# Weight sums of the folded products made by accumulating DMAs in DRAM, with signs that need only additions

## The chip, the cores and the metric

The kernel runs on one core of a Trainium2 chip. The metric is the device time of one execution in microseconds (us). The kernel before takes 1085.0 us, the median of three runs (1084.67 to 1085.46). Profiles show one execution; its lines name TensorE as PE (its weight loads as PEld), VectorE as DVE, ScalarE as ACT, GpSimd as POOL and SyncE as SP, which issues nearly all DMAs.

## The reference

One layer of an encoder on 512 tokens with 1024 channels, all in float32. The part that the change concerns comes last:

```
mixed = (g_ssd * y_ssd + g_attn * y_attn) @ w_o          # (512, 1024) @ (1024, 1024)
x = x + rmsnorm(mixed, post_mix_norm)
h = rmsnorm(x, pre_mlp_norm)
f = square(relu(h @ w_mlp_in)) @ w_mlp_out               # (512, 1024) @ (1024, 4096), (512, 4096) @ (4096, 1024)
x = x + rmsnorm(f, post_mlp_norm)
```

Before it stand an input projection, a state-space scan over 8 groups of heads in both directions (`ssd`), an attention over a window of 128 tokens either way, gates, and the two output projections of these branches.

## The kernel before, in words

**Products.** Activations are kept transposed, channels on the 128 partitions and 512 tokens along the row. For accuracy each float32 operand is split into a high part in the matmul's reduced format and a low part (what is left), and every product is made of three matmuls: high by high, high by low, low by high (`mm3`, L404, `mm`, L398). ACT makes the high part of a weight by a cast, and POOL or DVE the low part by a subtraction (L473 and L477 for weights that are used as they are; L1571 and L1575 in `fold`).

**Quanta.** The work is a list of quanta, in order. An ordinary quantum is one block of 128 output channels: 8 blocks of the sum by 3 matmuls of 128x512, 24 matmuls. Each has its weight chunk of 512 KB, which SP loads (L453) into one of three raw buffers `wr`; the parts go into rings `wh` and `wl`, three deep (`SPL`). `prefetch` (L481) splits and loads ahead. Anything else is hung on a position in this list by `at(q, fn)` (L427): q is the index of a quantum, and a half means behind it. Tiles of 128x512 come from a common store of 67 slots (`Slots`).

**Order.** The program is first written down in this order. Then a planner (`Planner`, L77) simulates it with a duration for each instruction (`duration`, L205), a serial DMA queue (`plan`, L264) and the dependencies between tiles (`depend`, L156), and fixes the order of each engine's instructions (`chain`, L498). TensorE takes what is first in the list and ready; the others take what is due first. An instruction that was written down through `held_back` (L1341) may not start before the matmul ahead of it in the list has started. The semaphores make each engine wait, in its order, for what it really needs.

**Folded products.** The output projection w_o (`mix_quanta`, L1366) and each quarter of the down projection of the MLP (`down_quanta`, L1604; four parts of 1024 rows) are products of 2 x 2 blocks. They are made with seven block products instead of eight, by a scheme of Strassen and Winograd: sums S1 to S4 of activation blocks (`mix_second`, L1276; `combine`, L1457) meet sums T1 to T4 of weight blocks of 512x512, and three groups of products, X, Y and Z, are accumulated in PSUM and added up into the output (`done`). Before, the weight sums are T3 = B22 − B12, T2 = T3 + B11, T1 = B22 − T2, T4 = B21 − T2, written over the raw tiles where they can be:

```
sub(r("B12"), r("B22"), r("B12"))
add(r("B11"), r("B12"), r("B11"))
...
sub(raw[n, k], *((r("B22"), r("B11")) if n == "T1" else (r("B21"), r("B11"))))
```

DVE makes them, for tiles of 128 rows. For the down parts `fold` (L1522) does so when an operand is due (`operand`, L1539): it loads the four blocks B11, B12, B21, B22 of a part once, 16 tiles of 256 KB, keeps them in slots until their last use, and makes 16 adds or subtracts (L1536, L1537). For w_o `stage_wo` (L1347) does so beforehand, in four steps hung on the quanta of the scan branch's output projection (`ssd_out_quanta`): 16 loads, 16 adds or subtracts (L1358 to L1361) and 16 stores of the sums into DRAM tiles `wot`; `fold` then loads the seven operands of w_o one by one.

**Stages in time.** To about 618 us: input projection, attention and scan, with gates and the attention's output projection between them. To about 690 us: the scan's output projection. To 744 us: w_o. Then the residual, norms and transposes (`mix_done`, `flip_h2`), under which the MLP begins: `up_halves` makes the first three blocks of the up projection for one half of the tokens and then for the other. From about 765 us ordinary up quanta, from about 793 us up quanta and folded down quanta in turn. From 1037 us the last folded products alone, and from 1070 us the last vector work and the stores.

Of the kernel before, what the change touches and what calls it, by code (L numbers as in the profile page):

```python
# [37 lines left out]
FETCH, STAGE = 2, 1  # L38
# [38 lines left out]
class Planner:  # L77
# [78 lines left out]
    def depend(self):  # L156
        self.pre = [set() for _ in self.ins]
        live, users, ring, seen, first, base = {}, {}, {}, {}, {}, {}
        self.turn = [set() for _ in self.ins]
        for n, i in enumerate(self.ins):  # L160
            for write, aps in ((False, i.ins), (True, i.outs)):
                for ap in self.operands(aps):
# [15 lines left out]
                    key = (name, ap.offset, tuple(map(tuple, ap.ap)))  # L178
# [26 lines left out]
    def duration(self, n):  # L205
# [22 lines left out]
        if e == "POOL":  # L228
            if "pow" in str(getattr(i, "op", "")):
# [34 lines left out]
    def plan(self, wait=0.3):  # L264
# [12 lines left out]
        for _ in self.ins:  # L277
# [21 lines left out]
            if e == "SP":  # L299
# [39 lines left out]
class Trunk:  # L339
# [936 lines left out]
    def mix_second(self, k):  # L1276
# [5 lines left out]
        tt(s[:, hi], b[:, hi], a[:, hi], op=ALU.add)  # L1282
# [4 lines left out]
        tt(t[:, hi], b[:, lo], s[:, lo], op=ALU.subtract)  # L1287
# [59 lines left out]
    def stage_wo(self, k):  # L1347

        nc = self.nc
        b = {}  # L1350
        for i in range(2):
            for j in range(2):
                b[i, j] = self.slots.get("wd")
                r0 = (4 * i + k) * 128
                nc.sync.dma_start(b[i, j], self.d_w_o[0, r0:r0 + 128, j * 512:(j + 1) * 512])
        t2, t1 = self.slots.get("wd"), self.slots.get("wd")
        tt = nc.vector.tensor_tensor
        tt(b[0, 1], b[1, 1], b[0, 1], op=ALU.subtract)  # L1358
        tt(t2, b[0, 1], b[0, 0], op=ALU.add)
        tt(t1, b[1, 1], t2, op=ALU.subtract)  # L1360
        tt(b[1, 0], b[1, 0], t2, op=ALU.subtract)  # L1361
        for n, t in (("T1", t1), ("T2", t2), ("T3", b[0, 1]), ("T4", b[1, 0])):
            nc.sync.dma_start(self.wot[n][k * 128:(k + 1) * 128], t)
        self.slots.put(t1, t2, *b.values())

    def mix_quanta(self):  # L1366
# [9 lines left out]
        def done(t, j, ps, _):  # L1376
# [11 lines left out]
    def mix_done(self, t, h2):  # L1388
# [6 lines left out]
        for j in range(2):  # L1395
            nc.scalar.activation(junk, h2[j], AF.Square, accum_out=ssq[:, j:j + 1])
            nc.vector.tensor_tensor(h2[j], h2[j], self.g2[j], op=ALU.mult)
# [59 lines left out]
    def combine(self, part, k):  # L1457
# [16 lines left out]
        tt(s[:, hi], b[:, hi], a21, op=ALU.add)  # L1474
# [3 lines left out]
        tt(t[:, hi], b[:, lo], s[:, lo], op=ALU.subtract)  # L1478
# [43 lines left out]
    def fold(self, steps, src, ops, held, done, lo, tags, staged=None):  # L1522
# [5 lines left out]
        uses = {"B11": ["B11"], "T2": ["B22", "B12", "B11"], "T1": ["B22", "B11"], "T4": ["B21", "B11"], "T3": ["B12"],  # L1528
                "B22": ["B22"], "B21": ["B21"]}
        if staged:  # L1530
            uses = {n: [n] for n in uses}
        order = [s[1] for s, _ in steps]
        at = lambda x: [i for i, n in enumerate(order) if x in uses[n]]
        need = {n: [x for x in uses[n] if order[at(x)[0]] == n] for n in order}
        over = {n: tuple(x for x in uses[n] if order[at(x)[-1]] == n) for n in order}
        sub = lambda c, a, b: nc.vector.tensor_tensor(c, a, b, op=ALU.subtract)  # L1536
        add = lambda c, a, b: nc.vector.tensor_tensor(c, a, b, op=ALU.add)  # L1537

        def operand(n, k):  # L1539

            r = lambda x: raw[x, k]
            free = over[n]
            if staged:
                return r(n), free
            if n == "T2":
                sub(r("B12"), r("B22"), r("B12"))
                add(r("B11"), r("B12"), r("B11"))
            if n in ("T1", "T4"):
                raw[n, k] = get("wt")
                sub(raw[n, k], *((r("B22"), r("B11")) if n == "T1" else (r("B21"), r("B11"))))  # L1550
                free += n,
            return r({"T2": "B11", "T3": "B12"}.get(n, n)), free

        def chunk(n, c):
            ks = 2 * c, 2 * c + 1

            def loads():
                for x in need[n]:
                    for k in ks:
                        raw[x, k] = get("wd")  # L1560
                        nc.sync.dma_start(raw[x, k], staged[x][k * 128:(k + 1) * 128] if x[0] == "T" else
                                          src(int(x[1]) - 1, int(x[2]) - 1, k))

            def make(ring):
# [3 lines left out]
                for i, k in enumerate(ks):  # L1568
                    w, free = operand(n, k)
# [6 lines left out]
                    put(*[raw.pop((x, k)) for x in free])  # L1576
# [5 lines left out]
        def product(a, b, bank, after, last):  # L1582

            def run(parts):
# [3 lines left out]
                for u in range(2):  # L1588
                    tok = slice(u * 128, (u + 1) * 128)
                    for c in [slice(0, 512)] if not last or u == 0 else [slice(0, 256), slice(256, 512)]:  # L1590
# [5 lines left out]
                        for t, j in after:  # L1596
                            done(2 * t + u, j, banks[bank][u], c)
# [6 lines left out]
    def down_quanta(self, part):  # L1604
# [11 lines left out]
        def done(t, j, ps, c):  # L1616
# [3 lines left out]
            else:  # L1620
                self.nc.vector.tensor_tensor(self.acc[t, j][:, c], self.acc[t, j][:, c], ps[:, c], op=ALU.add)  # L1621
# [124 lines left out]
```

## Time and profile before

| | |
|---|---|
| median of three runs | 1085.0 us |
| the profiled execution, as the program reports it | 1085.44 us |
| its span in the profile | 1083.7 us |
| granted TensorE clock | 0.997 |
| PE / DVE / ACT / POOL busy | 1073.5 / 785.1 / 654.4 / 808.1 us |
| DMA moved | 152.21 MB |

In a group of instructions the columns are: line, engine, operation, out<-in with shapes, count; busy us and mean ns; idle us of the engine just before them, and what ended it. A row of waits gives who waited for whom: us in total, times, longest. A piece of the chain of work that ended last, or of the timeline, gives start, length, what. A DMA issue gives the size of one and the median us from issue to landing.

### The profile page before, as it was taken

What the parts mean: (1) busy time and instruction counts of PE and PEld (TensorE: products, weight loads), DVE (VectorE), ACT (ScalarE), POOL (GpSimd) and SP (SyncE); (2) the same over time, 40 slices, a digit from 0 to 9 for tenths busy, and PEclk for the clock granted to TensorE, in tenths of its full rate; (3) what the DMA queues carried; (4) which work ended last, traced back from release to release, by engine and by line L of the source; (5) the groups of instructions that cost most, each with busy time, mean ns of one, the idle gap of its engine ahead of it and who ended that gap; (6) DMA issues with size and microseconds to landing.
All of it is one profiled execution on the core that took longest, in us unless ns stands there. A gap on an engine that the chain in (4) does not pass through costs nothing.

```text
span 1083.7 us, 16956 instructions
## 1 busy us (share of the span) xinstructions
PE 1073.5 (99%) x5584; PEld 902.2 (83%) x5584; DVE 785.1 (72%) x1345; ACT 654.4 (60%) x1407; POOL 808.1 (75%) x1011
## 2 busy tenths in 40 slices
PE   9999999999999999999999999999999999999997
PEld 8888888888888888888888888889888888888885
DVE  6578787788796787887877558668873755755787
ACT  5566776686865767676686522476755434434443
POOL 4446567557558898989898768566998978978844
PEclk9999999999999999999999999999999999999999
DMA  7444624625536555556564389754722612611522
GB/s 218 118 121 125 150 76 123 146 74 158 131 107 164 149 144 160 158 143 167 136 179 113 103 253 332 226 198 127 237 65 59 201 53 59 198 55 59 161 93 78
DMA packets 221000, 152.21 MB, mean 140 GB/s; under 512 B 12493, under 2 KB 194229, under 8 KB 220912
## 3 DMA queue, kind: packets, MB, share of 16 engines
q1 hardware_dynamic: 220764, 151.06, 48.6%
q8 instruction: 44, 0.72, 0.3%
q14 instruction: 44, 0.36, 0.1%
q10 hardware_dynamic: 148, 0.07, 0.0%
HBM read 138.19 MB, written 12.91 MB: 139 GB/s over the span
## 4 chain that ended last, share of the span: by engine, by line
PE 94%; DVE 2%; DMA 2%; ACT 1%; SPq 1%; issue 1%; POOL 0%; POOLq 0%; DVEq 0%
PE pp L398 66%; PE ps L398 25%; PE ps L402 3%; DMA x<-in_x 1%; DMA wr<-in_w_in 0%; ACT b L423 0%; DVE B L944 0%; DVE x L1401 0%; DVE P L855 0%; DVE x L1655 0%; DVE acc L1621 0%; SPq L383 0%; SPq L570 0%; DVE Q L832 0%; DVE ag L1648 0%
## 5 line engine op out<-in xcount | busy, mean ns | idle before, releaser
L398 PE MATMUL pp<-b,wh 128*128 128x512 f32 (+1 forms) x1840 | 564.8, 388 | 0.2 <-DVE b L424 0.2
L477 POOL TENSOR_TENSOR wl<-wr,wh 128x256 fp32r<-128x256 f32 (+1 forms) x503 | 418.2, 860 | 137.4 <-ACT wh L473 133.9
L398 PEld LDWEIGHTS pp<-b,wh 128*128 128x128 f32 x1840 | 340.2, 188 | 68.2 <-issue 1.5
L398 PE MATMUL pp<-b,wl 128*128 128x512 f32 (+1 forms) x920 | 356.5, 388 | 0.0
L398 PEld LDWEIGHTS pp<-b,wl 128*128 128x128 f32 x920 | 172.9, 188 | 34.3
L473 ACT CAST wh<-wr 128x1024 fp32r<-128x1024 f32 x131 | 136.5, 1042 | 82.0 <-PE pp L398 56.1
L1575 POOL TENSOR_TENSOR wl<-wd,wh 128x256 fp32r<-128x256 f32 x168 | 139.8, 862 | 39.9 <-ACT wh L1571 31.9
L1571 ACT CAST wh<-wd 128x512 fp32r<-128x512 f32 x108 | 63.2, 618 | 53.9 <-PE pp L398 23.8
L398 PE MATMUL ps<-wh,fh 128*128 128x512 f32 (+1 forms) x196 | 75.5, 385 | 0.5 <-DVE acc L1621 0.5
L398 PE MATMUL ps<-wl,fh 128*128 128x512 f32 (+1 forms) x196 | 75.5, 385 | 0.0
L398 PE MATMUL ps<-wh,fl 128*128 128x512 f32 (+1 forms) x196 | 75.4, 385 | 0.0
L1112 ACT ACTIVATE n<-cb,tables 128x128 f32<-128x128 f32 x128 | 48.8, 391 | 26.8 <-DVE cb L1103 22.8
L1449 DVE SCALAR_TENSOR_TENSOR pp<-pp,r 128x512 f32<-128x512 f32 (+1 forms) x31 | 17.5, 565 | 54.0 <-ACT r L1446 53.9
L1575 POOL TENSOR_TENSOR wl<-wt,wh 128x256 fp32r<-128x256 f32 x56 | 45.4, 844 | 9.9 <-ACT wh L1571 6.0
L944 DVE SCALAR_TENSOR_TENSOR u<-pp,cv,u 128x510 f32<-128x510 f32 (+1 forms) x64 | 47.6, 744 | 2.9 <-ACT u L940 1.7
L1042 POOL TENSOR_TENSOR xd<-x,tables 128x256 f32<-128x256 f32 x48 | 35.0, 747 | 19.5 <-ACT x L967 16.9
L1113 ACT ACTIVATE m<-cb,tables 128x128 f32<-128x128 f32 x128 | 48.7, 389 | 0.3 <-DVE cb L1103 0.3
L1148 POOL TENSOR_TENSOR w<-w,E 128x256 f32<-128x256 f32 x48 | 40.3, 852 | 11.1 <-DVE w L1144 5.4
L398 PEld LDWEIGHTS ps<-wh,fh 128*128 128x128 f32 x196 | 36.8, 188 | 8.1 <-DVE acc L1621 0.7
L1108 ACT ACTIVATE rf<-rf,tables 128x128 f32<-128x128 f32 x128 | 41.9, 393 | 2.6 <-DMA rf<-csT 2.6
L398 PEld LDWEIGHTS ps<-wl,fh 128*128 128x128 f32 x196 | 36.8, 188 | 7.4
L398 PEld LDWEIGHTS ps<-wh,fl 128*128 128x128 f32 x196 | 36.8, 188 | 7.2
(301 smaller groups left out, 2085.3 us busy)
## 6 DMA issues: line engine op xcount, KB each, us to landing
wr<-in_w_in SPq DMA_DIRECT2D x74, 512.0 KB, 4.8
wr<-in_w_mlp_in SPq DMA_DIRECT2D x32, 512.0 KB, 4.1
wd<-in_w_mlp_out SPq DMA_DIRECT2D x64, 256.0 KB, 4.7
rb<-csT SPq DMA_DIRECT2D x32, 256.0 KB, 3.9
rf<-csT SPq DMA_DIRECT2D x32, 256.0 KB, 5.5
wr<-in_w_ssd_out SPq DMA_DIRECT2D x14, 512.0 KB, 5.4
wd<-in_w_o SPq DMA_DIRECT2D x28, 256.0 KB, 4.6
E<-csE SPq DMA_DIRECT2D x96, 64.0 KB, 3.9
```

Of the source, the lines that this page charges most:

```text
L398: self.nc.tensor.matmul(out, lhsT, rhs, start=start, stop=stop, skip_group_check=more)
L402: self.nc.tensor.transpose(out, src, self.ident[:n, :n])
L473: self.nc.scalar.copy(hi[:, :m], raw)
L477: engines[e].tensor_tensor(lo[:, c], raw[:, c], hi[:, c].bitcast(F32), op=ALU.subtract)
L944: nc.vector.scalar_tensor_tensor(u[:, a:e], ps[:, a + d:e + d], self.wtap(t, b), u[:, a:e], op0=ALU.mult, op1=ALU.add)
L1042: nc.gpsimd.tensor_tensor(v4(xd[:, d * 256:(d + 1) * 256]), v4(xs(c)), by_dir(self.coef, c)[:, d].unsqueeze(2).to_broadcast([128, 4, 64]), ...
L1108: nc.scalar.activation(v4(rf)[:, h], v4(rf)[:, h], AF.Identity, bias=ncs[:, 0, h:h + 1])
L1112: nc.scalar.activation(v4(n)[:, h], cb[:, 0], AF.Copy, scale=dt[:, 0, h:h + 1])
L1113: nc.scalar.activation(v4(m)[:, h], cb[:, 1], AF.Copy, scale=dt[:, 1, h:h + 1])
L1148: nc.gpsimd.tensor_tensor(wc, wc, E[:, d], op=ALU.add)
L1571: nc.scalar.copy(hi, w)
L1575: (nc.vector if e == "v" else nc.gpsimd).tensor_tensor(low[:, q], w[:, q], hi[:, q].bitcast(F32), op=ALU.subtract)
```

## The change

The sums get other signs, so that each is an addition: T1 = B11 + B12, T3 = B12 + B22, T2 = T1 + B22, T4 = T2 + B21. The activation sums, the sign with which the Y products are added up, and the sign of the second half of the output's columns (taken back where the gain is multiplied in) follow. The sums are no longer made by DVE. A new function, `sums_in_dram`, makes them as whole blocks of 512x512 in DRAM: SP copies a block (1 MB, DRAM to DRAM), POOL issues a DMA that adds another block to it. For each matrix these are eight steps, each hung `pace` quanta behind the one before and held back there. The five matrices start at quantum 10 (w_o), at quantum 30 (down part 0), and at the first, the 15th and the 31st quantum of the MLP (parts 1, 2 and 3). `stage_wo` goes; `fold` loads all seven operands of a part one by one, T1 to T4 out of DRAM tiles. The planner gets a duration for a DMA issued by POOL and its place in the DMA queue, and a rule on the order of later writes of a tile. The core of the diff:

```diff
-                            if len(held) > 1:
-                                self.turn[n].add(first[held[-2]])
+                            if len(held) > 1:
+                                behind[name] = first[held[-2]]
...
+                    if write and name in behind:
+                        self.turn[n].add(behind[name])
...
         if e == "POOL":
+            if "DMA" in kind:
+                return 1200, False
...
+            elif e == "POOL" and "DMA" in type(self.ins[n]).__name__:
+                queue = max(queue, end + self.LEAD) + 2 * self.transfer(n)
+                free[e], end = end, queue + self.TAIL
...
-        tt(s[:, hi], b[:, hi], a[:, hi], op=ALU.add)
+        tt(s[:, hi], a[:, hi], b[:, hi], op=ALU.subtract)
         tt(s[:, lo], s[:, hi], a[:, lo], op=ALU.subtract)
...
-        tt(t[:, hi], b[:, lo], s[:, lo], op=ALU.subtract)
+        tt(t[:, hi], b[:, lo], s[:, lo], op=ALU.add)
...
-    def stage_wo(self, k):
...
+    def sums_in_dram(self, name, src, q, pace):
+        nc = self.nc
+        t = {f"T{i}": self.dp.tile([512, 512], F32, name=f"{name}t{i}") for i in range(1, 5)}
+
+        def copy(a, b):
+            return lambda: nc.sync.dma_start(t[a], src(*b) if type(b) is tuple else t[b])
+
+        def plus(a, b):
+            return lambda: nc.gpsimd.dma_start(t[a], src(*b), accum_op=ALU.add)
+
+        steps = [copy("T1", (0, 0)), plus("T1", (0, 1)), copy("T3", (0, 1)), plus("T3", (1, 1)),
+                 copy("T2", "T1"), plus("T2", (1, 1)), copy("T4", "T2"), plus("T4", (1, 0))]
+        for i, fn in enumerate(steps):
+            self.at(q + pace * i, lambda fn=fn: self.held_back(fn))
+        return t
...
-                self.nc.scalar.copy(acc[t, j], ps)
+                if minus:
+                    self.nc.scalar.activation(acc[t, j], ps, AF.Copy, scale=-1.0)
+                else:
+                    self.nc.scalar.copy(acc[t, j], ps)
...
-                self.nc.vector.tensor_tensor(acc[t, j], acc[t, j], ps, op=ALU.add)
+                self.nc.vector.tensor_tensor(acc[t, j], acc[t, j], ps, op=ALU.subtract if minus else ALU.add)
...
-            nc.vector.tensor_tensor(h2[j], h2[j], self.g2[j], op=ALU.mult)
+            if j:
+                nc.vector.scalar_tensor_tensor(h2[j], h2[j], -1.0, self.g2[j], op0=ALU.mult, op1=ALU.mult)
+            else:
+                nc.vector.tensor_tensor(h2[j], h2[j], self.g2[j], op=ALU.mult)
...
             def loads():
-                for x in need[n]:
-                    for k in ks:
-                        raw[x, k] = get("wd")
+                for k in ks:
+                    raw[n, k] = get("wd")
...
-                    w, free = operand(n, k)
+                    w = raw.pop((n, k))
...
+        half = lambda w, r0: lambda i, j: w[0, r0 + i * 512:r0 + (i + 1) * 512, j * 512:(j + 1) * 512]
+        down_sums = lambda p, *at: self.sums_in_dram(f"dn{p}", half(self.d_w_mlp_out, 1024 * p), *at)
+        self.wot = self.sums_in_dram("wo", half(self.d_w_o, 0), 10, 2.5)
+        self.dnt = {0: down_sums(0, 30, 2.5)}
...
-        for k in range(4):
-            self.at(c0 + STAGE + k, lambda k=k: self.held_back(lambda: self.stage_wo(k)))
...
+        self.dnt.update({1: down_sums(1, n(), 1.5), 2: down_sums(2, n() + 14, 2), 3: down_sums(3, n() + 30, 2)})
```

`combine` and `down_done` change in the same way as `mix_second` and `mix_done`.

More of the change, by code (lines that the diff above doesn't have):

```diff
@@ L157, in depend @@
         self.pre = [set() for _ in self.ins]
-        live, users, ring, seen, first, base = {}, {}, {}, {}, {}, {}
+        live, users, ring, seen, first, base, behind = {}, {}, {}, {}, {}, {}, {}
         self.turn = [set() for _ in self.ins]
@@ L1527, in fold @@
         raw, banks, turn = {}, {}, [0]
[L1528 to L1552, printed above, removed]
         def chunk(n, c):
@@ L1575, in make @@
                         (nc.vector if e == "v" else nc.gpsimd).tensor_tensor(low[:, q], w[:, q], hi[:, q].bitcast(F32), op=ALU.subtract)
-                    put(*[raw.pop((x, k)) for x in free])
+                    put(w)
                     made.append((hi, low))
@@ L1620, in done @@
             else:
[L1621 removed]
+                self.nc.vector.tensor_tensor(self.acc[t, j][:, c], self.acc[t, j][:, c], ps[:, c], op=ALU.subtract if minus else ALU.add)
             left[t, j] -= c.stop == 512
@@ L1626, in down_quanta @@
         ops = {k: self.f[part, k] for k in range(4)}
-        return self.fold([(s, part == 3) for s in steps], src, ops, self.held[part], done, LO_DOWN[part], dict.fromkeys("XYZ", "ps"))
+        return self.fold([(s, part == 3) for s in steps], src, ops, self.held[part], done, LO_DOWN[part], dict.fromkeys("XYZ", "ps"), self.dnt[part])
     def down_done(self, t, j, col):
```

39 lines of the change are left out of this document (13 added, 26 removed).

## The prediction

> **What bounds it.** I read the page's totals first, then the chain of waits, then who waited for whom on TensorE, then the busy time by stage.
>
> ```profile
> span 1083.7 us, 16956 instructions
> ...
> PE 1073.5 (99%) x5584; PEld 902.2 (83%) x5584; DVE 785.1 (72%) x1345; ACT 654.4 (60%) x1407; POOL 808.1 (75%) x1011
> ...
> PE 94%; DVE 2%; DMA 2%; ACT 1%; SPq 1%; issue 1%; POOL 0%; POOLq 0%; DVEq 0%
> ```
>
> TensorE (PE) is busy 1073.5 of 1083.7 us, so 10.2 us is all the idle time there is. The program prints 1085.44 us for this execution, 1.7 more than its span; the median of the three timed runs is 1085.0. Sums are made against 1085.44, and as the forecast is a difference I add it to the median.
>
> Busy matmul time can hide waiting, since ends are modelled. So I look at the waits and the pace:
>
> ```profile
> PE ps L398 <- DVE zero L560: 1.0, 1, 1.0
> PE ps L398 <- ACT b L415: 0.9, 1, 0.9
> PE ps L398 <- DVE acc L1621: 0.5, 1, 0.5
> PE pp L398 <- DVE b L424: 0.2, 1, 0.2
> 618.69 92.53 PE pp L398 x408
> ...
> 757.96 4.80 PE pp L398 x40
> ...
> 765.16 21.79 PE pp L398 x96
> ...
> 1037.19 32.65 PE ps L398 x144
> 1075.30 2.58 issue
> ```
>
> All waits of TensorE come to 2.6 us (1.0+0.9+0.5+0.2), 1.9 of it in the first 30 us, which the diff does not touch. The chain pieces say that the pace is full: 92.53 us / 408 = 226.8 ns in the gate and output projections, 21.79 / 96 = 227.0 ns in the MLP, 32.65 / 144 = 226.7 ns in its last part; 24 of them, a quantum, are 5.44 us. From 757.96 on there is no hole until the last matmul ends at 1037.19 + 32.65 = 1069.8. What is left is the tail, 1083.7 − 1069.8 = 13.9 us of vector work and stores behind that matmul. The change keeps every matmul. So it can gain only from these holes, and lose wherever a weight arrives late.
>
> ```profile
> 200.00:300.00 100.00, 100.00 (x617) 84.91 (x616) 78.98 (x170) 73.54 (x184) 63.63 (x83) 1.00 0.48 125
> ...
> 760.00:860.00 100.00, 100.00 (x463) 83.68 (x462) 63.90 (x106) 57.53 (x108) 94.28 (x129) 1.00 0.44 135
> 860.00:950.00 90.00, 90.00 (x399) 74.55 (x398) 56.87 (x91) 40.88 (x72) 78.62 (x99) 1.00 0.39 117
> 950.00:1040.00 90.00, 90.00 (x399) 74.56 (x398) 56.61 (x92) 41.03 (x73) 70.78 (x88) 1.00 0.28 85
> ```
>
> The columns are busy us of PE, PEld, DVE, ACT, POOL in each stage, then clock, DMA share, GB/s. POOL is the engine nearest to its limit: 94.28 of 100 us in the first MLP stage, 78.62 of 90 in the next, 70.78 of 90 in the third. DVE, the engine that the change relieves, is at 57 to 64%. DMA is at 0.28 to 0.44.
>
> **Removed: vector adds.**
>
> ```profile
> L1536 DVE TENSOR_TENSOR wt<-wd,wd 128x512 f32<-128x512 f32 x32 | 29.8, 935 | 7.9 <-POOL wl L1575 6.8 <-DMA wd<-in_w_mlp_out 1.0
> ...
> L1537 DVE TENSOR_TENSOR wd<-wd,wd 128x512 f32<-128x512 f32 x16 | 16.8, 1053 | 0.1
> ...
> L1536 DVE TENSOR_TENSOR wd<-wd,wd 128x512 f32<-128x512 f32 x16 | 15.5, 982 | 16.6 <-DMA wd<-in_w_mlp_out 14.4 <-POOL wl L477 2.2
> ...
> L1358 DVE TENSOR_TENSOR wd<-wd,wd 128x512 f32<-128x512 f32 x4 | 4.4, 1090 | 9.4 <-DMA wd<-in_w_o 9.4
> ...
> L1360 DVE TENSOR_TENSOR wd<-wd,wd 128x512 f32<-128x512 f32 x4 | 4.2, 1059 | 0.0
> L1359 DVE TENSOR_TENSOR wd<-wd,wd 128x512 f32<-128x512 f32 x4 | 4.1, 1030 | 0.1
> L1361 DVE TENSOR_TENSOR wd<-wd,wd 128x512 f32<-128x512 f32 x4 | 4.0, 989 | 0.0
> L1575 POOL TENSOR_TENSOR wl<-wd,wh x168: 729/742/1267, 682.6 to 1065.6; 128x256 fp32r<-128x256 f32 x168
> ```
>
> The sums of the four down parts are 64 adds: 29.8 + 16.8 + 15.5 = 62.1 us. Those of w_o are 16: 4.4 + 4.2 + 4.1 + 4.0 = 16.7 us. Together 78.8 us of DVE, and none of it on the path, since TensorE waited 0.2 us for such work after 618 us (the flip of h2, L424) and 0.5 for an accumulation. Direct gain: nothing, and at the very most those 0.7 us.
>
> There is an indirect gain on POOL. Its low-part pieces of one and the same shape take 729 to 1267 ns, median 742, and the removed adds take 677 at best, 935 to 1053 on average: the two engines lengthen each other. By the mean of 862 ns in the group of L1575 (quoted below), POOL loses 862 − 742 = 120 ns on each of 224 pieces, 27 us in all; the adds are one of several causes, so I book 10 us over the MLP. It is slack for POOL, not time.
>
> **Sign form.** Two adds become subtracts and two subtracts become adds, the Y products are subtracted instead of added, the first w_o accumulator may be copied with a scale, and the gain multiply of the j = 1 half is a scalar-tensor-tensor.
>
> ```profile
> L1655 DVE SCALAR_TENSOR_TENSOR x<-ag,frs,x 128x512 f32<-128x512 f32 x7 | 5.2, 747 | 0.4 <-POOL frs L1651 0.4
> ...
> L1397 DVE TENSOR_TENSOR h<-h,post_mix_norm 128x512 f32<-128x512 f32 x8 | 5.9, 736 | 1.9 <-ACT junk L1396 1.9
> ...
> L1575 POOL TENSOR_TENSOR wl<-wd,wh 128x256 fp32r<-128x256 f32 x168 | 139.8, 862 | 39.9 <-ACT wh L1571 31.9 <-PE ps L398 2.8 <-PE pp L398 2.0
> ```
>
> Those two forms cost 747 and 736 ns at 128x512, so 8 instructions differ by under 0.1 us in all. Zero. The raw weight tiles are given back one by one instead of being held over several products, so more slots are free for the weights ahead; the planner's new ordering rule (a later write of a tile also comes after the first use of the tile before it in its ring) adds no instruction.
>
> **Added: copies, accumulations, more loads.** For each of five matrices SP issues four 1 MB DRAM copies and POOL four 1 MB accumulating DMAs. SP loses 16 loads of w_o and 16 stores of 256 KB, and in the down parts it loads 7 operands of 1 MB instead of 4, 48 more loads of 256 KB.
>
> ```profile
> q1 hardware_dynamic: 35568, 27.79, 37.4%
> ...
> wr<-in_w_mlp_in SPq DMA_DIRECT2D x27, 512.0 KB, 4.2
> wd<-in_w_mlp_out SPq DMA_DIRECT2D x45, 256.0 KB, 5.0
> ```
>
> These rows are for 743 to 990 us, the stretch where the sums of parts 1, 2 and 3 are placed (from quantum n, n+14 and n+30 of the MLP, 5.44 us each). There 27.79 MB took 37.4% of 247 us on 16 engines, which is 301 GB/s at full use, 3.5 us for 1 MiB. Now 45 loads become 45 x 7/4 = 79, plus 8.9 MB: 36.7 MB or 122 us. Twelve copies at 3.5 are 42 us. The trace of before has no accumulation and no DRAM-to-DRAM copy. Lower bound: one pass, 3.5 us, twelve are 42. Upper bound by these rows: three passes (read, read, write), 126. I take two, 84 us, since a plain load is also one read with one write. Sum: 122 + 42 + 84 = 248 of 247 us, with bounds of 206 and 290. So the DMA engines go from 0.38 to about full in this stretch. The fit in the Trainium skill ("DMA: Bandwidth & Descriptors", Anatomy of one DMA) is lighter: 2.0 us plus the bytes at 436 GB/s, as an estimate 4.4 us for each accumulation, landing included. By it the sum would be 122 + 42 + 53 = 217; no run here shows it yet.
>
> What hides this is lead.
>
> ```profile
> 765.50 3.17 SPq L453 DMA_DIRECT2D wr<-in_w_mlp_in  x2
> ...
> 771.91 0.38 SPq L453 DMA_DIRECT2D wr<-in_w_mlp_in  x1
> 760.35 1.05 ACT L473 CAST wh<-wr 128x1024 fp32r<-128x1024 f32 x1 [0.16 <-issue]
> ...
> 771.74 1.05 ACT L473 CAST wh<-wr 128x1024 fp32r<-128x1024 f32 x1
> ...
> 787.59 1.04 ACT L473 CAST wh<-wr 128x1024 fp32r<-128x1024 f32 x1
> 759.84 2.01 POOL L1415 TENSOR_TENSOR eps<-eps,rst 128x1 f32<-128x1 f32 x1
> ...
> 762.09 8.97 POOL L477 TENSOR_TENSOR wl<-wr,wh 128x256 fp32r<-128x256 f32 x12
> ...
> 773.52 2.83 POOL L477 TENSOR_TENSOR wl<-wr,wh 128x256 fp32r<-128x256 f32 x4
> ```
>
> The tightest load of the MLP is the first of the two at 765.50: cast at 771.74, low part on POOL from 773.52, and its quantum begins at 765.16 + 3 x 5.44 = 781.5. With 1.05 for the cast and 0.71 (2.83 / 4) for the first piece it could be cast 8 us later; as ACT's and POOL's other work stands behind it, I count 5. The next load, at 771.91, is cast at 787.59, a lead of 15.7 us, and I take that for those after it. A 1 MB copy ahead of a load in SP's queue costs it 3.5 us, sharing with an accumulation perhaps as much again: covered after 772, hardly at 765. In the attention and scan stage two matrices add 8 copies and 8 accumulations, 8 x 3.5 + 8 x 7 = 84 us, over quanta 10 to 47, at least 37 x 5.44 = 204 us: 0.41 at most on top of 0.48. Covered. In the projection stage behind it the 32 transfers of w_o disappear, 8.4 MB or 28 us of DMA; TensorE did not wait there.
>
> The new waits: each accumulation waits at the head of POOL's queue until its copy has landed, with low parts behind it that TensorE needs; the copies out of T1 and T2 wait at the head of SP's queue until the accumulation has landed, with loads behind them that ACT's casts need. A 256 KB load lands after 5.0 us, 0.9 of it transfer at 301 GB/s, so landing adds 4.1. A copy takes 7.6, an accumulation 11.1 (7.6 to 14.6). The steps are 1.5 to 2.5 quanta apart, 8.2 to 13.6 us. So POOL finds its copy landed, and SP waits 3 us once, for T2 in part 1, where the step is 8.2. The leads take that up.
>
> **POOL's own price.** Twelve DMAs are issued by POOL between 743 and 990, eight earlier. No DMA of POOL's is in the trace.
>
> ```profile
> L453 SPq DMA_DIRECT2D wr<-in_w_in x74: 367/373/778, 15.2 to 588.9; - x74
> ```
>
> Below: SP spends 0.37 us on an issue. Above: 5.0 us, the whole landing of a load, if POOL stood still until then. The diff's planner books 1.2, which I take, being near the lower row. Twelve are 14 us, between 4 and 60, against 5.7 + 11.4 + 19.2 = 36 us of idle POOL in the three stages (100 − 94.28, 90 − 78.62, 90 − 70.78) and the 10 us of relief. It fits up to about 3.8 us each. The tight place is 760: the fourth weight block is cast at 760.35, POOL starts its low part at 762.09 and TensorE needs it at 765.16, and the first accumulation of part 1 is held back to just there (n + 1.5). With 0.71 for the first piece POOL may lose 765.16 − 762.80 = 2.4 us there before TensorE waits.
>
> **Sum.** Adds 0, sign form 0, DMA 0 under cover, POOL 0 to 1 at 760 us, and some tenths of replanning in the early stages, whose order comes out of the planner anew. I take +0.3: 1085.3 us. The likeliest case's own range is 1084 to 1087.
>
> **Rivals.** First, slower through the DMA queue. SP waits for an accumulation that takes longer than its step, and loads stand behind a full set of DMA engines. Place: part 1's sums, from 743 us on, where x1's stores, the first down loads and the up loads come together. For it: 248 of 247 us. Against it: leads of 15.7 us after 772. It decides when an accumulation takes over 8.2 + 5 = 13 us. Price at the upper bound: 290 − 247 = 43 us of backlog, of which the loads carry 122/290, 18 us; less the lead, 2; and 14.6 − 8.2 = 6 us of waiting SP in part 1: +8, 1093.0. The Trainium skill ("DMA: Bandwidth & Descriptors", Issuing engines are not separate DMA queues) has this as a rule: transfers that GpSimd issues run on the same 16 engines as SP's.
>
> Second, slower through POOL. If one DMA holds POOL for 4 us or more, the accumulation at 760 costs TensorE 4 − 2.4 = 1.6 us, and twelve of them, 48 us, eat the 46 of slack, 2 more: +4, 1089.0. Against it: the slack, and SP's 0.37. The Trainium skill ("SBUF — State Buffer", the box on SWDGE) speaks against the change here: GpSimd writes the descriptors itself, and a DVE instruction in a 2-port mode keeps it from that, 3.1 us instead of 0.62 in its example. At that price twelve are 37 us and this rival would not yet come about; no trace of before shows it.
>
> Third, faster. Relief of DVE and POOL and a planner that happens on a better order close holes and shorten the tail. The waits give 0.7 us, and the 13.9 us of the tail are adds, squares, a power and stores that stay; I put 1.8 on it. −2.5, 1082.5. The same goes for the case that the adds are moved as said but were never waited for: that is the forecast itself.
>
> **Numbers.** A measurement of this kernel can tell about 0.2%, 2.2 us, from no change. No change 0.58; slower by DMA 0.20, by POOL 0.12; faster 0.10. The range holds the forecast, the second rival and the lower half of the first, 0.80, and leaves out the third and the upper half of the first: 1083.0 to 1092.0.
>
> **What would show it.** Right: TensorE's waits still near 3 us, pieces of 226.7 ns without holes, DVE some 79 us lower, POOL's L1575 mean below 862 ns, DMA share at 743 to 990 above 0.8. Wrong: TensorE waiting for weights near 760 to 790, POOL idle behind a copy's landing, SP waiting at the copies out of T1 and T2, or a DMA share of 0.6, which would say that accumulations cost one pass.

## The result, and the profile after

The changed kernel takes 1095.88 us (median of four runs, 1095.4 to 1099.82) against 1085.23 for the kernel before on the same chip: a ratio of 1.0107, 95% interval 1.0083 to 1.0131. It is slower by 1.1%, where no change was forecast. The profiled execution took 1095.45 us, its span is 1093.7. The page's totals and DMA queues, then a row of stages (busy us of PE, PEld, DVE, ACT, POOL; clock; DMA share; GB/s) and the waits of TensorE:

```profile
PE 1077.6 (99%) x5584; PEld 902.2 (82%) x5584; DVE 718.1 (66%) x1265; ACT 653.5 (60%) x1407; POOL 797.9 (73%) x1031
...
q1 hardware_dynamic: 228668, 176.23, 54.5%
q0 software_dynamic: 10560, 20.97, 11.7%
```

```profile
743.00:990.00 247.00, 244.28 (x1152) 205.02 (x1152) 119.57 (x214) 125.99 (x237) 201.59 (x287) 0.99 0.90 245
```

```profile
PE pp L405 <- DVE ft L1487: 2.7, 1, 2.7
PE ps L405 <- DVE m L1122: 1.3, 1, 1.3
PE ps L405 <- DVE pT L888: 1.1, 2, 0.7
PE ps L405 <- DVE zero L567: 1.1, 1, 1.1
PE ps L405 <- ACT pT L888: 0.7, 1, 0.7
PE ps L405 <- DVE acc L1605: 0.5, 1, 0.5
PE ps L405 <- ACT b L422: 0.2, 1, 0.2
PE pp L405 <- ACT wv L587: 0.2, 1, 0.2
```

DVE is 67.0 us lower (785.1 to 718.1), POOL 10.2. DMA went from 0.38 to 0.90 in 743 to 990 us. TensorE has a wait that was not there, 2.7 us for `ft`, an instruction of the activation sums of the MLP's first blocks (`combine`), and three in the attention, 1.3 + 1.1 + 0.7. Apart from 0.2 us in its first 15 us (`wv`) it waits for no weight.

To see where the time came from I compare the start of the same matmul in two traces, by its number in TensorE's order of 5584 (in the attention the kinds of matmuls come in another order, so only points outside it are compared):

```
matmul number      800      2200      4200      4400      5584
before          144.78    372.76    764.40    809.23   1075.90
after           144.39    377.47    769.54    818.95   1085.63
difference       -0.39     +4.71     +5.14     +9.72     +9.72
```

So the loss has two pieces: 5.1 us between 145 and 373 us (the early loss), and 4.6 between 765 and 819 (the late loss). Behind that every matmul comes 9.7 later, at the old pace.

The late loss is seen whole in the chain that released each step of TensorE's wait (start, length, what), with the rows of POOL, DVE and TensorE at that time (start, length, engine, line, what, count). The last view is the group of the same DVE instruction in the kernel before (busy us, mean ns):

```profile
766.76 0.51 ACT r L1457
767.26 0.02 issue
767.29 0.44 DVE pp L1460
767.73 0.02 issue
767.76 0.42 DVE r L1460
768.18 6.26 DVE x L1415
774.45 0.62 DVE pp L1460
```

```profile
767.17 1.11 POOL L1363 DMA_DIRECT2D dn1t<-in_w_mlp_out  x1
767.93 5.96 POOL L484 TENSOR_TENSOR wl<-wr,wh 128x256 fp32r<-128x256 f32 x8
```

```profile
768.10 6.35 DVE L1415 SCALAR_TENSOR_TENSOR x<-h,rs,x 128x512 f32<-128x512 f32 x1
```

```profile
778.49 0.70 PE L405 MATMUL pp<-b,wh 128*128 128x512 f32 x2 [2.73 <-DVE ft L1487]
...
779.82 0.63 PE L405 MATMUL pp<-b,wl 128*128 128x512 f32 x1
780.25 1.06 PE L405 MATMUL pp<-b,wh 128*128 128x512 f32 x2
```

```profile
L1404 DVE SCALAR_TENSOR_TENSOR x<-h,rs,x 128x512 f32<-128x512 f32 x8 | 5.7, 742 | 0.0
```

POOL issues the first accumulation of part 1 at 767.17 and then runs eight low parts in one go, 767.93 to 773.89. At 768.10 DVE begins one update of the residual, `x<-h,rs,x`, which reads two tiles of 128x512 in SBUF (the on-chip memory). In the kernel before the eight of these took 742 ns on average; this one takes 6.35 us and ends at 774.45, just after POOL's run. DVE's next work, the first blocks' activation sums, comes late by as much. TensorE waits for one of these, L1487, which reads `pp`, the PSUM tile (PSUM holds the sums of products) that TensorE's next matmul writes. L1487 starts at 777.93. In the kernel before it (there L1476) started at 767.60 and ended 2.5 us before that matmul, so a part of the delay is taken up by slack. TensorE stops for 2.73 us. From start to start the hole is 3.11 us, 2.9 more than a matmul's 0.23. Five matmuls later the pace halves: seven come every 0.43 us (779.82 to 780.25 is the first), 1.4 more, and three around them every 0.31 to 0.33, 0.3 more. Together 4.6. The Trainium skill ("SBUF — State Buffer", Who interferes with whom) has the rule for it: a DVE instruction with two SBUF inputs and a GpSimd instruction that reads SBUF share one read path, and whoever comes second is blocked fully until the first is done. The trace agrees on who, and adds that it can last for a whole run of eight instructions.

The trace of before has two rows that belong beside this. There, too, one of these updates began inside a run of POOL's low parts (the run from 762.09 to 771.06), and it took its usual time. Later another DVE instruction with two SBUF inputs, whose own time is 0.68 us, took 3.35, beside a run of four low parts that began just ahead of it:

```profile
762.73 0.74 DVE L1404 SCALAR_TENSOR_TENSOR x<-h,rs,x 128x512 f32<-128x512 f32 x1
...
800.64 3.35 DVE L416 TENSOR_TENSOR fl<-ft,fh 128x512 fp32r<-128x512 f32 x1
```

```profile
800.62 2.82 POOL L1575 TENSOR_TENSOR wl<-wd,wh 128x256 fp32r<-128x256 f32 x4
```

TensorE did not wait for that one, and POOL issued no DMA in that kernel. So such a lock needs no DMA. What POOL's DMA certainly does is to set when the run behind it starts; whether it also makes the lock more likely is not shown.

### The profile page after: what moved, and what is told of

Its sections match the earlier page's. It is cut to its first block, busy times and chain, and to the rows that moved or that the text cites. A ratio compares the mean times of both kernels' runs of the same rounds, so it can differ in the third digit from the quotient of the medians.

```text
span 1093.7 us, 17001 instructions
## 1 busy us (share of the span) xinstructions
PE 1077.6 (99%) x5584; PEld 902.2 (82%) x5584; DVE 718.1 (66%) x1265; ACT 653.5 (60%) x1407; POOL 797.9 (73%) x1031
## 4 chain that ended last, share of the span: by engine, by line
PE 90%; DVE 6%; ACT 2%; issue 1%; POOL 0%; POOLq 0%; DVEq 0%; ACTq 0%
PE pp L405 62%; PE ps L405 25%; PE ps L409 2%; DVE P L877 1%; DVE x L1415 1%; DVE B L951 0%; ACT n L1119 0%; DVE P L862 0%; ACT m L1120 0%; ACT wh L480 0%; DVE yT L1194 0%; ACT P L871 0%; DVE m L1122 0%; DVE m L1121 0%; DVE u L951 0%
## 5 line engine op out<-in xcount | busy, mean ns | idle before, releaser
L484 POOL TENSOR_TENSOR wl<-wr,wh 128x256 fp32r<-128x256 f32 (+1 forms) x503 | 400.2, 836 | 141.2 <-ACT wh L480 137.9
L1559 POOL TENSOR_TENSOR wl<-wd,wh 128x256 fp32r<-128x256 f32 x224 | 176.6, 821 | 61.8 <-ACT wh L1555 41.4
L1555 ACT CAST wh<-wd 128x512 fp32r<-128x512 f32 x140 | 81.2, 618 | 73.3 <-PE pp L405 39.5
L1155 POOL TENSOR_TENSOR w<-w,E 128x256 f32<-128x256 f32 x48 | 41.7, 880 | 11.1 <-DVE w L1151 10.0
L1605 DVE TENSOR_TENSOR acc<-acc,ps 128x512 f32<-128x512 f32 (+1 forms) x49 | 32.9, 673 | 17.6 <-PE ps L405 17.2
```

The costliest lines, as they stand in the source:

```text
L484: engines[e].tensor_tensor(lo[:, c], raw[:, c], hi[:, c].bitcast(F32), op=ALU.subtract)
L1155: nc.gpsimd.tensor_tensor(wc, wc, E[:, d], op=ALU.add)
L1555: nc.scalar.copy(hi, w)
L1559: (nc.vector if e == "v" else nc.gpsimd).tensor_tensor(low[:, q], w[:, q], hi[:, q].bitcast(F32), op=ALU.subtract)
```

## The experiments

Three theories came first. A: DVE is kept out by POOL's run behind its DMA; that makes the late loss. B: the DMA engines, the queue or waits for the sums make the losses. C: it is another part of the change, the seven loads for four, the signs or the planner's new rule. The early loss then got pairs of its own: P and X, then O and T, told with their runs. The early and late step of each kernel are differences to before as above (early: from matmul 800 to 2200; late: 4200 to 4400). Each is one profiled execution against the one trace of before. What comes ahead of matmul 800 is in neither column: there traces of the same order differ by up to 1.9 us.

```
kernel              time (us)  ratio, 95% interval     early   late
after                1095.88   1.0107 (1.0083-1.0131)  +5.09   +4.58
no_sums              1085.37   1.0000 (0.9991-1.0010)  +0.05    0.00
copies_only          1086.54   1.0011 (1.0002-1.0021)  +0.75    0.00
plain_pool           1090.43   1.0051 (1.0036-1.0066)  +5.02    0.00
small_pool           1088.46   1.0034 (1.0021-1.0047)  +0.54   +4.16
early_only           1095.16   1.0086 (1.0058-1.0114)  +9.91    0.00
late_only            1091.57   1.0058 (1.0043-1.0073)  -0.01   +4.51
later_start          1092.40   1.0065 (1.0045-1.0084)  +6.56    0.00
blind_plan           1134.67   1.0464 (1.0438-1.0491) +11.11  +11.34
tiny_same_order      1094.87   1.0087 (1.0070-1.0104)  +4.32   +4.38
moved                1117.55   1.0298 (1.0283-1.0313)  -0.01    0.00
replaced_a           1086.92   1.0014 (1.0006-1.0023)  +0.96    0.00
replaced_b           1089.87   1.0047 (1.0035-1.0060)  -0.19    0.00
```

### no_sums: everything but the sums

```diff
...
-        for i, fn in enumerate(steps):
-            self.at(q + pace * i, lambda fn=fn: self.held_back(fn))
-        return t
+        return {"T1": src(0, 0), "T2": src(1, 1), "T3": src(0, 1), "T4": src(1, 0)}
```

> Left out: all sums in DRAM; where a sum would be read, the fold reads a plain block of the weight instead, so the products are of other matrices. Loads, signs and everything else as in the changed kernel. Theory A (a DMA issued by POOL lets the POOL work behind it hold the port that it shares with DVE, and DVE comes late): no such DMA is left, 1085 (1084 to 1086). Theory B (the DMA queue and the 16 engines are filled by copies and accumulations): the same, 1085, DMA share at 760 to 950 near 0.5. Theory C (the cost is in what else changed: 48 more loads, the order that the planner makes): 1091 or more.

1085.37 us, no difference. The 48 more loads, the sign form and the new planning rule cost nothing, and the removed adds bring nothing. Theory C falls. The loss comes with the 40 DMAs, or with the order that the planner makes for them.

### copies_only: the 20 copies without the 20 accumulations

```diff
-        def plus(a, b): ...
-        steps = [copy("T1", (0, 0)), plus("T1", (0, 1)), copy("T3", (0, 1)), plus("T3", (1, 1)), ...
+        steps = [copy("T1", (0, 0)), None, copy("T3", (0, 1)), None, ...
...
```

> Left out: the accumulations; the four copies of each matrix stay at their places, so the sums are copies of single blocks. Theory A: no DMA of POOL's, 1085 to 1087, DVE's longest two-input instruction under 3.4 us. Theory B: 20 of 40 transfers stay and the loads stand behind them in SP's queue: 1088 to 1091, about half of the loss.

+0.1%: with 20 MB of copies in SP's queue, and the order planned for them, TensorE loses 0.75 us in the attention and 0.44 more by 765. The bytes of the copies alone are not it.

### plain_pool and small_pool: POOL's DMAs as plain copies, and as 32 KB copies without SP's

```diff
-            return lambda: nc.gpsimd.dma_start(t[a], src(*b), accum_op=ALU.add)
+            return lambda: nc.gpsimd.dma_start(t[a], src(*b))
```

> The accumulations become plain copies issued by POOL, at the same places, with the order on all engines the same as in the changed kernel; so the sums are single blocks. Theory A: nothing changes, 1094 to 1098, and the DVE instruction near 768 us is again locked out for 5 us or more. Theory B: a plain copy reads half as much, lands some 4 us earlier, and the loss falls to a half or less: 1087 to 1091.

```diff
-            return lambda: nc.gpsimd.dma_start(t[a], src(*b), accum_op=ALU.add)
+            return lambda: nc.gpsimd.dma_start(t[16 * i:16 * i + 16], src(*b)[0:16])
...
```

> Left out: the sums, as in the run without sums; POOL only issues a copy of 32 KB to a scratch in DRAM at each of the 20 places of an accumulation, SP copies nothing. Theory A: slow, 1088 to 1096, with POOL's pieces overlapping behind its DMAs and DVE locked out at one or more places. Theory B: 1085 to 1086, as the DMA engines carry under 1 MB more.

The two split the loss. With plain 1 MB copies by POOL the early loss is whole (5.02) and the late one gone; with 32 KB copies, no sums and no copies of SP's it is the other way round (0.54 and 4.16). DVE in the kernel with plain copies, and POOL and DVE in the one with small copies:

```profile
768.29 0.73 POOL L1363 DMA_DIRECT2D dn1t<-in_w_mlp_out  x1
769.04 9.14 POOL L484 TENSOR_TENSOR wl<-wr,wh 128x256 fp32r<-128x256 f32 x11
```

```profile
769.22 1.17 DVE L1415 SCALAR_TENSOR_TENSOR x<-h,rs,x 128x512 f32<-128x512 f32 x1
```

```profile
762.32 0.62 POOL L1360 DMA_DIRECT2D dn1t<-in_w_mlp_out  x1
762.97 5.61 POOL L484 TENSOR_TENSOR wl<-wr,wh 128x256 fp32r<-128x256 f32 x8
```

```profile
762.91 0.42 DVE L1458 SCALAR_TENSOR_TENSOR r<-pp,r 128x256 f32<-128x256 f32 x1
763.25 5.88 DVE L1413 SCALAR_TENSOR_TENSOR x<-h,rs,x 128x512 f32<-128x512 f32 x1
```

With 32 KB a DMA the same DVE instruction is kept out for 5.88 us, so for the late loss the traffic is not needed: theory B falls there. With the plain copies it took 1.17, and POOL's pieces took 0.83 each instead of 0.70: the engines alternated. So at this place the lock is there where the loss is, and not where it isn't. What lets DVE in with the plain copies, though POOL's pieces begin just as close behind the DMA (0.75 us against 0.76), stays open.

### early_only, late_only and later_start: the losses apart, and the late one moved

```diff
-        self.dnt.update({1: down_sums(1, n(), 1.5), 2: down_sums(2, n() + 14, 2), 3: down_sums(3, n() + 30, 2)})
+        for p in (1, 2, 3):
+            b = half(self.d_w_mlp_out, 1024 * p)
+            self.dnt[p] = {"T1": b(0, 0), "T2": b(1, 1), "T3": b(0, 1), "T4": b(1, 0)}
```

> Only the sums of w_o and of down part 0 are made; parts 1 to 3 read plain blocks in the place of T1 to T4, so their output is not the product (work left out: 12 copies and 12 accumulations). If the two losses of the changed kernel are separate: +5.0 before 360 us stays, nothing at 765 us, time 1090 to 1091. If the late loss were a result of the early one (another order or phase), +9, 1094 to 1095.

```diff
-        self.wot = self.sums_in_dram("wo", half(self.d_w_o, 0), 10, 2.5)
-        self.dnt = {0: down_sums(0, 30, 2.5)}
+        b, d = half(self.d_w_o, 0), half(self.d_w_mlp_out, 0)
+        self.wot, self.dnt = {"T1": b(0, 0), "T2": b(1, 1), "T3": b(0, 1), "T4": b(1, 0)}, {}
+        self.dnt[0] = {"T1": d(0, 0), "T2": d(1, 1), "T3": d(0, 1), "T4": d(1, 0)}
```

> Only the sums of down parts 1, 2 and 3 are made; w_o and part 0 read plain blocks in the place of T1 to T4 (work left out: 8 copies and 8 accumulations). If the two losses are separate: nothing before 743 us, +4.2 to +4.6 at 760 to 790 us with one DVE instruction of two SBUF inputs taking 5 us or more behind a DMA of POOL's: 1089 to 1090. If the late loss is a matter of phase alone, it may vanish: 1085 to 1086, and then no DVE instruction over 3 us at that place.

```diff
-        self.dnt.update({1: down_sums(1, n(), 1.5), ...
+        self.dnt.update({1: down_sums(1, n() + 4, 1.5), ...
```

> As the changed kernel, but the sums of part 1 start four quanta (21.8 us) later, so that no DMA of POOL's stands among the norms and transposes at 760 to 775 us. Theory A (DVE kept out by POOL's run behind its DMA at 768 us costs 4.6 us): no DVE instruction over 3 us there, +5 before 360 us and nothing after, 1090 to 1092. Theory B (the DMA engines' load costs it): the same bytes come with other loads and the loss stays, 1094 to 1097.

The losses are separate: early 9.91 and late 0 in the first, −0.01 and 4.51 in the second. Hanging part 1's sums four quanta later takes the late loss away, with the same bytes, and the same DVE instruction takes 0.90 us:

```profile
769.69 0.90 DVE L1415 SCALAR_TENSOR_TENSOR x<-h,rs,x 128x512 f32<-128x512 f32 x1
```

Theory A holds. What was not expected is the size of the early loss, 9.91 and 6.56 with engines that run the same order as in the changed kernel up to 355 us; the four runs of the first reach from 1091.33 to 1097.58. It has a part that varies from one execution to the next; the profiled one (1097.53) is among the slow ones.

### blind_plan: the planner does not know of the sums

```diff
+        if e == "SP" and outs[0].tensor.name.startswith(("wot", "dn0t", "dn1t", "dn2t", "dn3t")):
+            return 0, False
...
-                return 1200, False
+                return 0, False
...
```

> All 20 copies and 20 accumulations are issued as in the changed kernel, but the planner books no time for them, on POOL, on SP or in its DMA queue; so the order of the other instructions comes out as if there were no sums. Theory P (the 5 to 6 us that the changed kernel and the one with plain POOL copies lose before 360 us come from the order that the planner makes when it books the sums): early loss under 1.5 us, last matmul of the scan stages as before; time 1085.5 to 1090.5, by whether the lock at 768 us recurs (0 or +4.6). Theory X (the transfers themselves, or waits for them, cost those 5 us): the early loss stays at 5 or more, time 1090 to 1096.

Both theories missed: the time rose to 1134.67. With an order made as if the sums were free, TensorE loses 11.1 us in the attention, 4.2 from there to the MLP, and 33 in it (11.34 up to matmul 4400, 21.95 behind it). One of these places, on DVE and on POOL:

```profile
919.84 8.98 DVE L427 TENSOR_TENSOR fl<-fs,fh 128x512 fp32r<-128x512 f32 x1
```

```profile
919.09 0.98 POOL L1367 DMA_DIRECT2D dn2t<-in_w_mlp_out  x1
919.76 5.80 POOL L1563 TENSOR_TENSOR wl<-wd,wh 128x256 fp32r<-128x256 f32 x8
925.24 3.03 POOL L488 TENSOR_TENSOR wl<-wr,wh 128x256 fp32r<-128x256 f32 x4
```

The lock again, 8.98 us behind POOL's DMA and its twelve pieces, and this time it is an `fl` (the low part of an activation sum) that a folded product waits for (TensorE 5.4 us). The planner books such a lock for the length of one instruction (`port` in `plan`), so an order that takes account of POOL's DMAs may go round some of them; that is argued, not shown. The run says that the booking is needed; it doesn't say what the booked order costs.

### tiny_same_order: the planned order of the changed kernel with 1/32 of its bytes

```diff
-        size = 4 * math.prod(d[1] for d in dst.ap)
+        size = 2 ** 20 if dst.tensor.name.startswith(("wot", "dn0t", ...)) else 4 * math.prod(d[1] for d in dst.ap)
...
-            return lambda: nc.gpsimd.dma_start(t[a], src(*b), accum_op=ALU.add)
+            return lambda: nc.gpsimd.dma_start(t[a][0:16], src(*b)[0:16], accum_op=ALU.add)
...
```

> Every instruction stands in the same order as in the changed kernel on every engine (the planner books the sums as 1 MB each), but each copy and each accumulation moves only 16 rows, 32 KB; fold reads plain blocks in the place of T1 to T4 (left out: 31 of 32 parts of the sums). Theory O (the early 5 us lie in the order that the planner made): they stay, 4.5 us or more before 360 us. Theory T (the sums' own traffic on the DMA engines makes other loads land late): under 1.5 us before 360 us. At 768 us, theory A (POOL's run behind its DMA keeps DVE out, whatever the DMA moves): one DVE instruction over 5 us and +4 to +4.6 there; if it needs the megabyte, none. Time by O and A 1094 to 1096, by T and A 1089 to 1091, by T without A 1085 to 1087.

The early loss stays at 4.32 (4.5 or more was expected), the late one at 4.38. Theories O and A hold, T falls as the main cause. DVE's row, and the DMA share of 145 to 355 us, which is below that of before (0.48 in the same stretch):

```profile
768.60 6.12 DVE L1415 SCALAR_TENSOR_TENSOR x<-h,rs,x 128x512 f32<-128x512 f32 x1
```

```profile
145.00:355.00 210.00, 206.98 (x1289) 174.32 (x1288) 167.32 (x344) 148.08 (x358) 141.94 (x184) 1.00 0.45 121
```

The part that varies goes with late loads. The loads of the rotary tables (`rf<-csT`) feed the scan; this is what ACT waited for them in 140 to 360 us, in this kernel and in the one with the early sums alone, and a piece of the latter's chain:

```profile
ACT rf L1115 <- DMA rf<-csT: 3.1, 2, 2.6
```

```profile
ACT rf L1115 <- DMA rf<-csT: 8.4, 2, 4.9
```

```profile
251.71 7.20 DMA rf<-csT
```

Same order, 3.1 us against 8.4, and an early loss of 4.32 against 9.91 (5.5 and 5.09 in the changed kernel, 5.3 and 5.02 with plain copies by POOL, 7.1 and 6.56 in later_start). That the waits make the difference is argued from these five: in the kernel without sums, whose order is another, ACT waited 4.5 us for the tables and TensorE lost nothing.

The order itself shows in TensorE's holes. Two of them, 1.0 and 1.6 us from start to start, stand in all five kernels (at 251.6 and 337.3 us in the changed kernel), where the kernel before has no hole (TensorE is busy 210.00 us of 145 to 355); others come and go. A third, 0.8 to 1.0 us at 189.4, is in the four kernels with accumulations. The chain leads to it from a DVE instruction, a scaling of attention weights, that runs beside four of POOL's low parts behind an accumulation:

```profile
184.25 2.64 DVE L877 TENSOR_SCALAR P<-P,sm 128x256 f32<-128x256 f32 x1
```

With plain copies by POOL, in the same order, it takes 0.94 us, and the step of TensorE there is 0.18. So some 0.6 to 0.9 us of the early loss is DVE kept out by POOL, too.

### moved, replaced_a and replaced_b: the sums elsewhere

```diff
-        self.wot = self.sums_in_dram("wo", half(self.d_w_o, 0), 10, 2.5)
-        self.dnt = {0: down_sums(0, 30, 2.5)}
+        self.wot = self.sums_in_dram("wo", half(self.d_w_o, 0), 50, 2.5)
+        self.dnt = {0: down_sums(0, 70, 2.5)}
```

(and part 1 at n() + 4, here and in the next two)

> The changed kernel with all its sums, placed elsewhere: w_o at quanta 50 to 67.5 and down part 0 at 70 to 87.5 (scan of the later groups, some 430 to 630 us, where the changed kernel lost nothing), part 1 four quanta later, parts 2 and 3 as they are. It computes the whole reference. If both losses belong to their places: no loss before 360 us, none at 768 us, 1084.8 to 1086.5, no more than 0.15% from the kernel before. If the sums cost TensorE wherever they run (bytes, POOL's time): 1088 to 1093.

A miss: 1117.55. Nothing is lost before 373 us and nothing in the MLP, but 31.7 us in the scan of the later groups, 26.4 of it in two holes, with a lower clock in these stretches (0.91 in 500 to 560 us, 0.86 in 560 to 620):

```profile
PE ps L405 <- DVE m L1122: 15.0, 1, 15.0
PE ps L409 <- DVE B L958: 11.4, 1, 11.4
```

So the places where the changed kernel lost nothing are not places where sums are free: the planner makes a new order for the whole stage, and this one is worse. It had said so itself. The planner ends with a length for its own order (`self.length`, L334): 1080.0 us for the kernel before, 1080.15 without sums, 1080.7 with the copies alone, 1086.2 for the changed kernel (1084.57 with its early sums only), 1130.4 here. It is no measurement, but the early loss stands in it: 1084.57 − 1080.15 = 4.4, and 4.32 was measured without the traffic. So I chose two placements with a short length:

```diff
+        self.wot = self.sums_in_dram("wo", half(self.d_w_o, 0), 6, 2)
+        self.dnt = {0: down_sums(0, 34, 2)}
```

> The changed kernel, whole reference computed, with its sums hung elsewhere: w_o from quantum 6 at a pace of 2 (was 10, 2.5), part 0 from quantum 34 at 2 (was 30, 2.5), part 1 four quanta later; parts 2 and 3 as they were. The length that the planner's simulation gives to its own order is 1080.0 us for the kernel before, 1086.2 for the changed one, 1130.4 for the one with the sums in the scan of the later groups, and 1080.5 here. Theory O (the early loss lies in the order, and the planner's length shows it) with theory A (no lock once POOL's DMA is off 768 us): 1085 to 1086.5. If the sums' traffic or POOL's time costs TensorE whatever the order: 1089 to 1093.

```diff
+        self.wot = self.sums_in_dram("wo", half(self.d_w_o, 0), 14, 2)
+        self.dnt = {0: down_sums(0, 86, 1.5)}
```

> As the run beside it, but w_o from quantum 14 at a pace of 2 and part 0 from quantum 86 at 1.5, among the gate and projection quanta of 618 to 690 us. The planner's length is 1080.6 us. Theory O with theory A: 1085 to 1086.5, and no more of TensorE's time lost at 620 to 690 us than 0.5. If the sums' traffic or POOL's time costs TensorE whatever the order: 1088 to 1093.

The first takes 1086.92 against 1085.19 (1.0014, 1.0006 to 1.0023), a little over what was expected. With the same 40 DMAs it keeps 1.7 of the 10.7 us. The second takes 1089.87, a miss: it lies in the range given for traffic or POOL's time. It loses nothing in the attention (−0.19) but 3.86 us by 722, in w_o, where ACT waited for a sum of w_o out of DRAM, loaded while an accumulation of part 0 was under way (697.8 to 711.7):

```profile
ACT wh L1555 <- DMA wd<-wot: 6.2, 1, 6.2
```

That is like the prediction's first rival, smaller and at another place; that the accumulation made the load late is argued, and the planner's length (1080.6) had not shown it. No version beats the kernel before: TensorE has no hole that the removed adds could fill.

## Why the prediction was wrong

**What held.** TensorE was the bound and the adds were worth nothing: DVE falls to 709.7 us without sums and the time does not move. The sign form and the extra loads cost nothing. POOL's price of a DMA, taken as 1.2, is 0.92 to 1.22 us, and the landing of an accumulation, taken as 11.1, is 11.5:

```profile
L1363 POOL DMA_DIRECT2D wot<-in_w_o x4: 1032/1116/1222, 107.0 to 214.4; - x4
...
L1363 POOL DMA_DIRECT2D dn2t<-in_w_mlp_out x4: 919/992/1018, 850.8 to 915.5; - x4
...
DMA to landing us min/median/max: 9.1/11.5/14.5
```

The landing of the fit in the Trainium skill ("DMA: Bandwidth & Descriptors", Anatomy of one DMA), 4.4 us as an estimate, is not what this kernel shows. For the load of the engines the fit was nearer: 0.90 of 247 us is 222, where the sum had 248 and the fit 217 (the last of the twelve accumulations came at 997, behind this stretch). L1559, which was L1575, has a mean of 821 ns (862 before), so POOL was relieved as said. SP never waited at a copy out of T1 or T2, where 3 us were booked, and TensorE waited for no load of the MLP. One reading of before was off, without weight for the sum: the last matmul starts at 1075.90, so the tail behind it is 7.5 us and not 13.9.

**What failed** is the sum, at "DMA 0 under cover, POOL 0 to 1 at 760 us, and some tenths of replanning in the early stages".

The tight place was found, and priced wrongly. The step asked how late POOL would come to TensorE, 1.2 of 2.4 us of slack, and POOL was in time. It had no term for what POOL's run, shifted to just behind its DMA, does to DVE. The prediction saw that the two engines lengthen each other, but booked that only as slack for POOL; the 3.35 us at 800.64 stood in the trace of before. One DVE instruction went from 0.74 to 6.35 us; the price was 4.6 us instead of 0 to 1. The second rival had the place and, with +4, nearly the size, but another mechanism: its condition, 4 us of POOL for a DMA, did not come about (1.1). The page of the Trainium skill that it named, "SBUF — State Buffer", was read in one direction only, DVE keeping GpSimd from its descriptors, while another of its rules (Who interferes with whom), GpSimd keeping out a DVE instruction with two SBUF inputs, is the one that the trace shows.

The early stage was called covered by DMA shares (0.48 + 0.41). The share stayed below that sum, 0.67 in 145 to 355, and TensorE still lost 5.1 us: 4.3 of it stays in the same order with 1/32 of the bytes, where the sum had some tenths (this holds the 0.6 to 0.9 of the lock at 184 us). The rest goes with late loads. That loads of this stage have no lead stood in the profile of before, where ACT waited three times for the tables in 140 to 360 us:

```profile
ACT rf L1108 <- DMA rf<-csT: 1.2, 3, 0.5
```

The lead of 15.7 us that was taken from the MLP holds there alone. The first rival's +8 is near to the total, but it put it on the MLP's loads, and TensorE waited for none of these.

The sum was +0.3 and the range ended at 1092.0; the traces show 4.6 + 5.1 = 9.7, of 10.0 us between the two profiled executions.

## What to carry to other kernels

Moving work from an idle engine to a queue gains nothing where the bound has no holes, and each DMA that POOL issues shifts a run of POOL's own instructions: look which DVE instructions with two SBUF inputs stand beside that run, and who waits for them. Where an order is fixed by a planner, a few added instructions change the order of a whole stage; its own length before and after is worth reading first (here it told the early loss and the 1117.55 us, but neither the lock nor the loss of the last placement), and hanging the same DMAs elsewhere brought back 9 of 10.7 us. A covered share of the DMA engines says nothing of loads with little lead: look at the lead in the very stage.

## What the runs showed of the hardware

- A DVE instruction with two SBUF inputs was kept out by a run of eight to twelve POOL pieces for 5.88, 6.12, 6.35, 6.48 (late_only) and 8.98 us, where 0.7 is its own time; in other runs at the same place the two engines alternated (0.90 to 1.17). In the kernel before a run of four, with no DMA, did it for 3.35 us.
- On POOL an accumulating DMA of 1 MB from DRAM to DRAM is recorded with 0.92 to 1.22 us in the changed kernel and a plain copy with 0.62 to 0.85 (plain_pool); the accumulation lands after 9.1 to 14.5 us, the copy after 6.3 to 9.7.
- Behind a hole of 2.73 us, from the fifth matmul on, TensorE made seven matmuls at half its pace; the mean granted clock of 760 to 790 us is 0.94. In small_pool, tiny_same_order and late_only six or seven followed holes of 2.26, 2.50 and 2.86 us. The Trainium skill ("TensorE: Matmul & The Clock Gate", Part 1) has this, with an idle window of about 3.4 us; here holes recorded as shorter sufficed.

```profile
760.00:790.00 30.00, 27.27 (x151) 23.49 (x149) 25.88 (x44) 19.10 (x43) 20.42 (x42) 0.94 0.94 251
```
